# An expert layer's weights in units of 256 rows by 1024 columns, the expert width in two halves, and the small splits pinned behind weight splits

## The chip, the cores and the metric

The kernel runs on one core of one Trainium2 chip. The metric is the device time of one execution in microseconds (us). A core has five engines that run their own instruction streams in order: PE (TensorE, matrix products and transposes), DVE (VectorE), ACT (ScalarE), POOL (GpSimd) and SP (SyncE, which issues transfers here). They wait for each other through semaphores; 16 DMA engines move data between the chip's memory (DRAM) and the on-chip memory (SBUF). PE writes its sums into PSUM, which has banks of 512 f32 numbers in each of 128 partitions.

## The reference

One encoder block: a mixer (Fourier, convolution, gates, output projection), then a mixture of experts, then a norm. The change touches the experts alone. Shapes: 1024 tokens, model width 1024, 16 experts of width 2048; each expert picks the 128 tokens with its highest router probabilities.

```python
def expert_choice_moe(h, w_router, b_router, w_gate_e, w_up_e, w_down_e):
    b, s, d = h.shape
    cap = EC_CAPACITY * s // N_EXPERTS
    ...
    vals, idx = lax.top_k(jnp.swapaxes(probs, 1, 2), cap)
    xe = jax.vmap(lambda hb, ib: hb[ib])(h, idx)
    a = jnp.einsum('becd,edf->becf', xe, w_gate_e)
    u = jnp.einsum('becd,edf->becf', xe, w_up_e)
    y = jnp.einsum('becf,efd->becd', jax.nn.silu(a) * u, w_down_e)
    y = y * vals[..., None].astype(y.dtype)
    ...
```

The result is added to x, multiplied by a gate (gate_f), and a final RMS norm with the gain g_final follows. All weights are f32, and every expert reads 24 MB of them.

## The kernel before

**The work.** From 775.8 us to 1930 us of the profiled execution the program runs the experts, one after the other. Products are made in three parts for precision: a weight w is split into whi (ACT rounds it to a shorter format, L92, 128x1024 numbers at a time) and wlo = w - whi (DVE, L93); the token rows are split alike into xh and xl, the hidden rows into hth and htl. PE then adds whi·xh, whi·xl and wlo·xh (`mm3x`, L1300 to L1302; L106, L109 and L112 for the down weights).

**Units and chunks.** Weights come in units of 1 MB, issued by SP (`fetch`, L1120) into a ring of 12 buffers as soon as a buffer is free. A unit is two *chunks* of 128x1024. An expert has 48 chunks (16 gate, 16 up, 16 down), and each chunk gives PE six products of 512 columns, 288 in an expert. This text numbers the chunks of an expert c0 to c47. There are six buffers each for whi and wlo (NWB), so the split of chunk n+6 must wait until PE has finished chunk n; a split engine can be at most six chunks ahead of PE.

**The order before.** The width of 2048 is worked in four quarters of 512 (`fc`): a gate product into PSUM tile a, an up product into u (each one bank, two buffers), ACT's Silu of a, DVE's multiplication by u (h, L1244). Then `put` transposes the four 128-column pieces of h on PE into tp (L1205), which ACT and DVE split into hth and htl, and `down` adds the quarter's four chunks into y (two banks). Gate and up units hold 512 rows by 512 columns, down units 256 rows by 1024. During an expert, the next expert's tokens are found: `pick` compares positions (oh, L1068, DVE), makes indices by eight small products (L1075, PE), copies them (r, idx), and POOL gathers the rows (L1087); `turn` transposes them (L1104) and splits them into xh and xl, which the next expert's first products read. `ys` (L1269) scales an expert's result, which POOL adds to the rows in DRAM. In the first two experts (e0, e1) DVE also does the router's search for the other 14 (L1006 to L1052). In the last (e15), three units of down weights are used without a split, as plain f32 products (L1222), and the final norm of the rows not picked is done beside it (`final`, ACT's squares at L1313).

**What sets the order.** A scheduler of the language orders each engine's instructions by program order and priorities; `issue_after(i)` keeps an instruction behind instruction i, where that is written. Before, the multiplication h, the splits of transposed tiles and ys are not pinned.

Of the kernel before, what the change touches and what calls it, by code (L numbers as in the profile page):

```python
# [15 lines left out]
P = 128  # L16
# [12 lines left out]
NSH = 0  # L29
NCMP = 2  # L30
FIN = ((10, 0), (8, 2), (6, 4), (4, 6))
# [49 lines left out]
class Block:  # L81
# [578 lines left out]
    def rstd(self, pool, ss, name):  # L660
        nc = self.nc
        n = ss.shape[1]
        ms = pool.tile([P, n], F32, name=name + "ms")
        nc.vector.tensor_scalar(ms, ss, 1.0 / D, EPS, op0=OP.mult, op1=OP.add)
        rs = pool.tile([P, n], F32, name=name + "rs", bufs=2)
        nc.gpsimd.tensor_tensor(rs, ms, self.neghalf[:, 0:n], op=OP.pow)
        return rs
# [395 lines left out]
    def pick(self, pool, e):  # L1063
# [16 lines left out]
        if not e:  # L1080
            self.warm(lambda: self.pau.tile([P, 512], F32, name="u"), 22)
# [57 lines left out]
    def plain(self, rows):  # L1139

        raw = self.take().rearrange("p (i k n) -> p i k n", i=2, k=rows // 2)
        for i in range(2):
            yield raw[:, i]
            if i:
                self.fetch()
            self.step()

    def unit(self, rows):

        raw = self.take()  # L1150
        nc = self.nc
        for i in range(2):
            hi = self.wsp.tile([P, 1024], F32R, name="whi")
            lo = self.wsp.tile([P, 1024], F32R, name="wlo")
            src = raw[:, 1024 * i:1024 * i + 1024]
# [4 lines left out]
            elif self.npop < NWB:  # L1160
                with self.tc.issue_after(self.hold):
                    self.split(hi, lo, src)
            else:
                self.split(hi, lo, src)
            self.npop += 1
            if i:
                if self.npop <= NWS:
                    with self.tc.issue_after(self.gather):
                        self.fetch(nc.gpsimd)
                else:  # L1170
                    self.fetch()
            self.pin = self.last
            self.step()
            yield hi.rearrange("p (k n) -> p k n", k=rows // 2), lo.rearrange("p (k n) -> p k n", k=rows // 2)

    def expert(self, pool, e, picked, side):
# [6 lines left out]
        y = self.py.tile([P, D], F32, name="y")  # L1183

        def up(fc, name):
            ps = self.pau.tile([P, 512], F32, name=name)
            k = 0
            for b in range(2):
                for j, (wh, wl) in enumerate(self.unit(4)):
                    if self.npop > NWB and (j == 0 or self.ranked < 2):  # L1190
                        with self.tc.issue_after(self.hold):
                            next(side, None)
                    for i in range(2):
                        self.mm3x(ps, (xh[:, k, :], xl[:, k, :]), (wh[:, i, :], wl[:, i, :]), k == 0, k == KD - 1)
                        k += 1
                if self.left:
                    self.left.pop()()
            return ps

        def put(fc):  # L1200

            pt = self.ptp.tile([P, 4, P], F32, name="tp")
            h = hs.pop(fc)
            for i in range(4):
                nc.tensor.transpose(pt[:, i, :], h[:, i * P:(i + 1) * P], self.ident)  # L1205
            hf = None
            if last and fc in (1, 2):
                hf = pool.tile([P, 4, P], F32, name="htf")
                nc.scalar.activation(hf, pt, AF.Copy)
                if fc == 2:  # L1210
                    ht[fc] = (None, None, hf)
                    return
            hh = pool.tile([P, 4, P], F32R, name="hth", bufs=2)
            hl = pool.tile([P, 4, P], F32R, name="htl", bufs=2)
            self.split(hh, hl, pt)
            ht[fc] = (hh, hl, hf)

        def down(fc, b):
            if last and (fc, b) in ((1, 1), (2, 0), (2, 1)):
                for i, w in enumerate(self.plain(2)):  # L1220
                    for n in (0, 512):
                        nc.tensor.matmul(y[:, n:n + 512], lhsT=ht[fc][2][:, 2 * b + i, :], rhs=w[:, 0, n:n + 512],  # L1222
                                         start=False, stop=False)
                return
            for i, (wh, wl) in enumerate(self.unit(2)):
                if i == 0:
                    next(side, None)
                f = 4 * fc + 2 * b + i
                self.mm3([y[:, 0:512], y[:, 512:1024]], [t[:, 2 * b + i, :] for t in ht[fc][0:2]],
                         [(wh[:, 0, n:n + 512], wl[:, 0, n:n + 512]) for n in (0, 512)],  # L1230
                         first=(f == 0), last=(f == 15))

        for fc in range(4):
            pa = up(fc, "a")
            if last and fc == 0:
                self.gl = pool.tile([P, D], F32, name="ys")
                nc.gpsimd.dma_start(out=self.gl, in_=self.io["g_final"].rearrange("(o d) -> o d", o=1)
                                    .partition_broadcast(P))
            if fc:
                put(fc - 1)  # L1240
            pu = up(fc, "u")
            h = pool.tile([P, 512], F32, name="h", bufs=2)
# [258 lines left out]
```

## Time and profile before

| what | value |
|---|---|
| three runs | 1945.67, 1948.66, 1950.64 us; median 1948.66 us |
| profiled execution | 1944.46 us, span 1942.6 us |
| mean granted TensorE clock | 0.992 of full speed |
| PE busy | 1888.7 us, 97% of the span |
| DVE busy | 1583.4 us, 82% |
| ACT busy | 1117.6 us, 58% |
| experts e0 to e15 | 775.8 to 1930.2 us |

The span is the profiled execution from its first to its last instruction; the 1.9 us that its own time has beyond it lie around it. A matmul's busy time includes time in which it waits in PE's pipeline, so a PE that is 97% busy can still be held up; what a product costs is read from the distance of two starts.

### The profile page before, as it was taken

The page shows a single profiled execution, that of the slowest core. Times are in us where ns is not written, and L with a number is a line of the kernel's source. Part 1 is how long each engine was busy: PE and PEld are TensorE (multiplying, and loading weights), DVE is VectorE, ACT ScalarE, POOL GpSimd, SP SyncE. Part 2 cuts the span into 40 slices and gives each one's busy share as a digit, 9 for nine tenths or more (in the row PEclk, how much of TensorE's full clock was granted, in tenths as well). Part 3 has the DMA queues.
Part 4 walks back from the last instruction along what each step waited for, and adds up shares of the span by engine and source line. Part 5 has one row for each costly group of instructions (what it writes and reads, how often), then busy time and mean ns, then how long its engine had stood idle before and what let it go on. Part 6 is the DMA issues. An engine that isn't in the chain of part 4 may idle for free.

```text
span 1942.6 us, 23945 instructions
## 1 busy us (share of the span) xinstructions
PE 1888.7 (97%) x8777; PEld 1507.7 (78%) x8777; DVE 1583.4 (82%) x2005; ACT 1117.6 (58%) x1403; POOL 136.2 (7%) x124
## 2 busy tenths in 40 slices
PE   6999999999999999999999999999999999999996
PEld 5788888777788877777888777777778778777873
DVE  5976678676853767999999898898998999989886
ACT  5533233433510433776787777777767777677764
POOL 1000000000130111000000000000000000000001
PEclk9999999999999999999999999999999999999998
DMA  8322224465774842999999999999999999999993
GB/s 298 128 67 65 87 76 154 143 228 195 232 250 140 291 180 108 396 367 346 378 372 389 354 359 376 372 364 360 392 364 355 386 366 361 380 373 355 392 367 135
DMA packets 244746, 549.02 MB, mean 283 GB/s; under 512 B 12644, under 2 KB 51652, under 8 KB 244628
## 3 DMA queue, kind: packets, MB, share of 16 engines
q1 hardware_dynamic: 229248, 494.50, 69.8%
q0 software_dynamic: 14528, 52.75, 8.6%
q8 instruction: 69, 1.13, 0.2%
q10 hardware_dynamic: 852, 0.24, 0.1%
q14 instruction: 49, 0.40, 0.1%
HBM read 507.61 MB, written 39.86 MB: 282 GB/s over the span
## 4 chain that ended last, share of the span: by engine, by line
PE 76%; DVE 12%; DMA 5%; issue 4%; ACT 2%; POOL 0%; ACTq 0%; POOLq 0%; DVEq 0%
PE pb L315 9%; DVE wlo L93 7%; PE pa L315 6%; PE pc L315 6%; PE u L1302 5%; PE u L1300 5%; PE u L1301 5%; PE y L106 5%; PE y L109 4%; PE y L112 4%; PE a L1302 4%; PE a L1301 4%; PE a L1300 4%; DMA raw<-in_w_up_e_dram 3%; PE mm L106 3%
## 5 line engine op out<-in xcount | busy, mean ns | idle before, releaser
L93 DVE TENSOR_TENSOR wlo<-raw,whi 128x1024 fp32r<-128x1024 f32 x759 | 889.0, 1218 | 61.1 <-ACT whi L92 52.5
L92 ACT ACTIVATE whi<-raw 128x1024 fp32r<-128x1024 f32 x759 | 751.4, 1052 | 61.2 <-PE y L112 21.6
L1302 PE MATMUL a<-wlo,xh 128*128 128x512 f32 x512 | 206.2, 403 | 7.0 <-DVE wlo L93 5.7
L1302 PE MATMUL u<-wlo,xh 128*128 128x512 f32 x512 | 203.6, 398 | 2.4 <-DVE wlo L93 2.4
L1300 PE MATMUL u<-whi,xh 128*128 128x512 f32 x512 | 202.5, 395 | 1.6 <-ACT whi L92 1.6
L1300 PE MATMUL a<-whi,xh 128*128 128x512 f32 x512 | 201.5, 394 | 1.9 <-ACT whi L92 1.6
L1301 PE MATMUL a<-whi,xl 128*128 128x512 f32 x512 | 201.8, 394 | 0.0
L1301 PE MATMUL u<-whi,xl 128*128 128x512 f32 x512 | 201.8, 394 | 0.0
L109 PE MATMUL y<-wlo,hth 128*128 128x512 f32 x496 | 161.3, 406 | 0.5 <-DVE wlo L93 0.3
L106 PE MATMUL y<-whi,hth 128*128 128x512 f32 x496 | 159.5, 402 | 0.0
L112 PE MATMUL y<-whi,htl 128*128 128x512 f32 x496 | 156.4, 396 | 0.0
L92 ACT ACTIVATE wh<-s 128x512 fp32r<-128x512 f32 x80 | 50.3, 631 | 135.9 <-PE pc L315 76.0
L1302 PEld LDWEIGHTS a<-wlo,xh 128*128 128x128 f32 x512 | 96.4, 188 | 39.3 <-DVE wlo L93 19.8
L1302 PEld LDWEIGHTS u<-wlo,xh 128*128 128x128 f32 x512 | 96.3, 188 | 31.1 <-DVE wlo L93 8.0
L1300 PEld LDWEIGHTS a<-whi,xh 128*128 128x128 f32 x512 | 96.7, 189 | 21.9 <-ACT whi L92 2.5
L1301 PEld LDWEIGHTS a<-whi,xl 128*128 128x128 f32 x512 | 96.5, 188 | 22.0 <-DVE xl L93 0.4
L1300 PEld LDWEIGHTS u<-whi,xh 128*128 128x128 f32 x512 | 96.5, 188 | 21.0 <-ACT whi L92 2.6
L1301 PEld LDWEIGHTS u<-whi,xl 128*128 128x128 f32 x512 | 96.6, 189 | 20.5
L112 PEld LDWEIGHTS y<-whi,htl 128*128 128x128 f32 x496 | 93.4, 189 | 22.5
L106 PEld LDWEIGHTS y<-whi,hth 128*128 128x128 f32 x496 | 91.8, 189 | 20.9 <-issue 0.5
L109 PEld LDWEIGHTS y<-wlo,hth 128*128 128x128 f32 x496 | 89.9, 190 | 20.4 <-DVE wlo L93 2.4
L1243 ACT ACTIVATE h<-a 128x512 f32<-128x512 f32 x64 | 38.2, 596 | 106.6 <-PE a L1302 106.6
(530 smaller groups left out, 3183.1 us busy)
## 6 DMA issues: line engine op xcount, KB each, us to landing
raw<-in_w_gate_e_dram SPq DMA_DIRECT2D x126, 1024.0 KB, 7.2
raw<-in_w_up_e_dram SPq DMA_DIRECT2D x126, 1024.0 KB, 9.1
raw<-in_w_down_e_dram SPq DMA_DIRECT2D x126, 1024.0 KB, 8.1
ld<-in_w_ada_dram SPq DMA_DIRECT2D x48, 512.0 KB, 5.4
ld<-in_w_in_dram SPq DMA_DIRECT2D x44, 512.0 KB, 4.4
sg_d<-q POOLq DMA_DIRECT2D x8, 1024.0 KB, 6.1
ld<-sg_d SPq DMA_DIRECT2D x16, 512.0 KB, 4.9
x<-in_x_dram SPq DMA_DIRECT2D x8, 512.0 KB, 3.3
```

The lines of the kernel that those rows point to most:

```text
L92: a = self.nc.scalar.activation(hi, src, AF.Copy).ins
L93: self.last = a, self.nc.vector.tensor_tensor(lo, src, hi, op=OP.subtract).ins
L106: nc.tensor.matmul(o, lhsT=lh, rhs=rh, start=first, stop=False)
L109: nc.tensor.matmul(o, lhsT=lh, rhs=rl, start=False, stop=False)
L112: nc.tensor.matmul(o, lhsT=ll, rhs=rh, start=False, stop=last)
L315: nc.tensor.matmul(o, lhsT=x[:, k, :], rhs=y[:, k, :], start=first and k == 0 and i == 0, stop=last and k == 3 and i == 2, skip_group_chec ...
L1243: nc.scalar.activation(h, pa, AF.Silu)
L1300: nc.tensor.matmul(o, lhsT=lhs[0], rhs=rhs[0], start=first, stop=False, **kw)
L1301: nc.tensor.matmul(o, lhsT=lhs[1], rhs=rhs[0], start=False, stop=False, **kw)
L1302: nc.tensor.matmul(o, lhsT=lhs[0], rhs=rhs[1], start=False, stop=last, **kw)
```

## The change

All units become 256 rows by 1024 columns (`self.ulist`). The expert width is worked in two halves of 1024: gate half 0 in c0 to c7, up half 0 in c8 to c15, gate half 1 in c16 to c23, up half 1 in c24 to c31, then all of down in c32 to c47. Tiles a and u are two banks wide with one buffer each. `products` lets one set of token or hidden columns act on both 512-column halves of a chunk before the next set. `next` and `half` keep a queue of six split chunks ahead of the products. Silu, the multiplication h, the splits of transposed tiles and ys are put off by one or two chunks (`put_off`) and then pinned behind the splits made by then (`pinned`). Two quarters of transposes stand in c22, two in c38; the pick at c26; the turn at c42 (TURN) and c43. In the last expert the three plain units come in one run, and the multiplication of the last columns by g_final stands behind the norm's factor. `fetch` follows when a unit's second chunk has been split, or when a plain unit has been used.

```diff
-FIN = ((10, 0), (8, 2), (6, 4), (4, 6))
+FIN = ((8, 0), (7, 2), (5, 4), (4, 6))
+PLAIN = ((1, 1), (2, 0), (2, 1))
...
+        self.late = [(n - 1, f) for n, f in self.late]
+        due = [f for n, f in self.late if n <= 0]
+        self.late = [(n, f) for n, f in self.late if n > 0]
+        for f in due:
+            self.pinned(f)
+
+    def pinned(self, f):
+        with self.tc.issue_after(self.pin[0]), self.tc.issue_after(self.pin[1]):
+            return f()
...
+    def next(self):
+
+        while len(self.queue) < NWB and self.nunit < len(self.plan):
+            self.half()
+        self.nused += 1
+        return self.queue.pop(0)
...
+        def products(o, lhs, w, first, end):
+
+            wh, wl = w
+            for i, (x, y) in enumerate(((lhs[0], wh), (lhs[1], wh), (lhs[0], wl))):
+                for a, b in cols:
+                    nc.tensor.matmul(o[:, a:b], lhsT=x, rhs=y[:, a:b], start=first and i == 0, stop=end and i == 2)
...
+            self.put_off(1, split)
...
+            pa = up("a", gaps[0])
+            h = pool.tile([P, D], F32, name="h")
+            hs[f] = h
+            self.put_off(1, lambda: nc.scalar.activation(h, pa, AF.Silu))
+            pu = up("u", gaps[1])
+            self.put_off(1, lambda: nc.vector.tensor_tensor(h, pu, h, op=OP.mult))
...
+        gate_up(0, ({}, {0: gain} if last else {}))
+        gate_up(1, ({3: lambda: put(0), 4: lambda: put(1), 6: rows if last else lambda: None}, {}))
...
+            if k == 0 and not last:
+                picking()
+            if k in (3, 6):
+                put(2 + k // 6)
+            if k == TURN and not last:
+                hold["next"] = self.turn(pool, *hold["next"])
...
-            dn = [("w_down_e", e, 256 * b, 256 * b + 256, 0, D) for b in range(8)]
-            for f in range(4):
-                self.ulist += [(n, e, 512 * b, 512 * b + 512, 512 * f, 512 * f + 512)
-                               for n in ("w_gate_e", "w_up_e") for b in range(2)]
+            self.ulist += [(n, e, 256 * b, 256 * b + 256, D * f, D * f + D) for f in range(2)
+                           for n in ("w_gate_e", "w_up_e") for b in range(4)]
+            self.ulist += [("w_down_e", e, 256 * b, 256 * b + 256, 0, D) for b in range(8)]
...
-        gpau, self.pau = pool("pau", bufs=2, space=PSUM)
+        gpau, self.pau = pool("pau", space=PSUM)
```

On DVE, in a whole expert of the steady part (e8, from ys to the next expert's ys), the order before is this. The names are those above; xN at the end is N such instructions in a row.

```order
L1269 SCALAR_TENSOR_TENSOR ys<-y,val,gf 128x1024
L93 TENSOR_TENSOR wlo<-raw,whi 128x1024 x7
L1244 TENSOR_TENSOR h<-u,h 128x512
L93 TENSOR_TENSOR wlo<-raw,whi 128x1024 x3
L93 TENSOR_TENSOR htl<-tp,hth 128x512
L93 TENSOR_TENSOR wlo<-raw,whi 128x1024 x2
L1077 COPY r_11730<-tp 128x5
L1083 SCALAR_TENSOR_TENSOR idx<-r_11730 128x1
L1093 TENSOR_REDUCE val<-r_11730 128x1
L1068 TENSOR_TENSOR oh<-pos,slot 128x1024
L93 TENSOR_TENSOR wlo<-raw,whi 128x1024 x3
L1244 TENSOR_TENSOR h<-u,h 128x512
```

The first h stands behind the split of c8, although the product u that it reads ends with PE's c7; ys stands between the splits of c1 and c2. With the change the same stretch of DVE reads:

```order
L1305 SCALAR_TENSOR_TENSOR ys<-y,val,gf 128x1024
L95 TENSOR_TENSOR wlo<-raw,whi 128x1024 x15
L1264 TENSOR_TENSOR h<-u,h 128x1024
L95 TENSOR_TENSOR wlo<-raw,whi 128x1024 x4
L95 TENSOR_TENSOR htl<-tp,hth 128x512
L95 TENSOR_TENSOR wlo<-raw,whi 128x1024
L95 TENSOR_TENSOR htl<-tp,hth 128x512
L95 TENSOR_TENSOR wlo<-raw,whi 128x1024
L1079 COPY r_11245<-tp 128x5
L1085 SCALAR_TENSOR_TENSOR idx<-r_11245 128x1
L95 TENSOR_TENSOR wlo<-raw,whi 128x1024 x2
```

Here ys stands behind the split of c6, and h behind that of c21, whose buffer is free only when PE has finished c15, the last chunk of u; the second h stands in the same way behind c37. The copy r stands behind c27, and its eight small products on PE at the end of c26.

The second place is DVE in e1, where the router's search ends and the tokens of e2 are picked. Before:

```order
L1052 TENSOR_TENSOR pos<-pos,po_2_7361 128x8x14
L93 TENSOR_TENSOR wlo<-raw,whi 128x1024
L1068 TENSOR_TENSOR oh<-pos,slot 128x1024
L93 TENSOR_TENSOR wlo<-raw,whi 128x1024
L1077 COPY r_7369<-tp 128x5
L93 TENSOR_TENSOR wlo<-raw,whi 128x1024
L1083 SCALAR_TENSOR_TENSOR idx<-r_7369 128x1
```

The splits in these rows are those of c29, c30 and c31; PE's small products for this pick stand in c28, its turn of the rows in c44. With the change:

```order
L1054 TENSOR_TENSOR pos<-pos,po_2_7530 128x8x14
L95 TENSOR_TENSOR wlo<-raw,whi 128x1024
L1070 TENSOR_TENSOR oh<-pos,slot 128x1024
L95 TENSOR_TENSOR wlo<-raw,whi 128x1024
L1079 COPY r_7567<-tp 128x5
L95 TENSOR_TENSOR wlo<-raw,whi 128x1024
L1085 SCALAR_TENSOR_TENSOR idx<-r_7567 128x1
L1095 TENSOR_REDUCE val<-r_7567 128x1
```

They are now the splits of c38, c39 and c40; PE's small products stand in c39, the turn begins in c42.

The third place is ACT in the last expert, beside the first plain products. Before, from the Silu ahead of them:

```order
L1243 ACTIVATE h<-a 128x512
L92 ACTIVATE whi<-raw 128x1024 x3
L1313 ACTIVATE oh,ss_16244<-raw 128x1024
L92 ACTIVATE whi<-raw 128x1024
L1313 ACTIVATE oh,ss_16244<-raw 128x1024
L1209 ACTIVATE htf<-tp 128x512
L92 ACTIVATE whi<-raw 128x1024
L1313 ACTIVATE oh,ss_16285<-raw 128x1024
L92 ACTIVATE whi<-raw 128x1024
L1313 ACTIVATE oh,ss_16285<-raw 128x1024
L92 ACTIVATE whi<-raw 128x1024 x2
L1243 ACTIVATE h<-a 128x512
```

The copy htf reads transposes that PE makes between plain products, and the splits of the next gate chunks (c30 on) stand behind it and between squares. With the change:

```order
L1262 ACTIVATE h<-a 128x1024
L94 ACTIVATE whi<-raw 128x1024 x3
L1357 ACTIVATE oh,ss_16101<-raw 128x1024
L94 ACTIVATE whi<-raw 128x1024
L1357 ACTIVATE oh,ss_16101<-raw 128x1024
L94 ACTIVATE whi<-raw 128x1024
L1357 ACTIVATE oh,ss_16130<-raw 128x1024
L94 ACTIVATE whi<-raw 128x1024
L1357 ACTIVATE oh,ss_16130<-raw 128x1024
L94 ACTIVATE whi<-raw 128x1024 x2
L1357 ACTIVATE oh,ss_16183<-raw 128x1024 x2
L1357 ACTIVATE oh,ss_16210<-raw 128x1024
```

The last two splits in these rows are those of c36 and c37; behind them PE has its twelve plain products, and the next split (c38) follows two copies of transposes.

## Rows read from the trace of the kernel before

**Rows 1.** The page: busy time, share of the span, instructions.
```profile
PE 1888.7 (97%) x8777; PEld 1507.7 (78%) x8777; DVE 1583.4 (82%) x2005; ACT 1117.6 (58%) x1403; POOL 136.2 (7%) x124
```

**Rows 2.** Windows of e0, e1, e3, e4, e6, e15: five engines' busy, clock, DMA, GB/s.
```profile
775.80:849.60 73.80, 73.68 (x401) 57.79 (x402) 72.20 (x115) 55.76 (x59) 1.32 (x1) 1.00 1.04 394
849.60:928.40 78.80, 75.57 (x372) 58.88 (x371) 75.69 (x104) 55.25 (x58) 5.43 (x2) 0.96 0.98 349
...
997.80:1067.10 69.30, 69.30 (x321) 56.59 (x320) 63.92 (x63) 53.41 (x58) 3.86 (x2) 1.00 1.03 376
1067.10:1137.20 70.10, 69.64 (x322) 56.34 (x320) 61.73 (x62) 49.60 (x57) 3.62 (x2) 1.00 1.00 357
...
1208.20:1279.20 71.00, 70.27 (x322) 56.10 (x321) 64.10 (x64) 51.48 (x59) 3.62 (x2) 1.00 1.01 369
...
1846.40:1930.20 83.80, 76.43 (x299) 54.48 (x297) 66.49 (x67) 52.69 (x69) 8.46 (x7) 0.96 0.77 282
```

**Rows 3.** Waits of PE's weight loads, e5 to e13: total us, times, longest.
```profile
PEld a L1302 <- DVE wlo L93: 14.2, 27, 0.9
```

**Rows 4.** Timeline of DVE in e9: start, us, instruction, idle time before.
```profile
1422.56 1.28 DVE L1269 SCALAR_TENSOR_TENSOR ys<-y,val,gf 128x1024 f32<-128x1024 f32 x1
...
1433.15 0.69 DVE L1244 TENSOR_TENSOR h<-u,h 128x512 f32<-128x512 f32 x1 [0.44 <-PE u L1302]
```

**Rows 5.** DVE's groups in e6: busy us, mean ns | idle before.
```profile
L93 DVE TENSOR_TENSOR wlo<-raw,whi 128x1024 fp32r<-128x1024 f32 x49 | 56.9, 1217 | 3.8 <-ACT whi L92 3.8
L1244 DVE TENSOR_TENSOR h<-u,h 128x512 f32<-128x512 f32 x4 | 2.8, 691 | 1.7 <-PE u L1302 1.7
L1068 DVE TENSOR_TENSOR oh<-pos,slot 128x1024 bf16<-128x1024 f32 x1 | 1.2, 1218 | 0.0
```

**Rows 6.** Timeline of PE in e3, a stretch without waits.
```profile
1051.65 0.39 PE L1302 MATMUL u<-wlo,xh 128*128 128x512 f32 x1
...
1054.40 0.40 PE L1302 MATMUL u<-wlo,xh 128*128 128x512 f32 x1
...
1057.79 0.72 PE L106 MATMUL y<-whi,hth 128*128 128x512 f32 x2
1058.35 0.63 PE L109 MATMUL y<-wlo,hth 128*128 128x512 f32 x2
...
1063.02 0.62 PE L112 MATMUL y<-whi,htl 128*128 128x512 f32 x2
```

**Rows 7.** Timeline of PE in the output projection, ahead of the experts.
```profile
737.65 0.63 PE L109 MATMUL mm<-wol,zh 128*128 128x512 f32 x2
...
739.94 0.39 PE L106 MATMUL mm<-woh,zh 128*128 128x512 f32 x1
```

**Rows 8.** The pick in e1: timelines of PE, DVE, POOL; a window; gather transfers.
```profile
895.75 0.38 PE L1075 MATMUL tp<-v,oh 128*128 128x5 bf16 x8 [2.85 <-DVE oh L1068]
...
897.96 0.15 DVE L1083 SCALAR_TENSOR_TENSOR idx<-r 128x1 int32<-128x1 f32 x1
...
898.87 3.04 POOL L1087 DMA_INDIRECT xg<-h_d,idx  x1 [43.62 <-issue]
...
896.00:902.00 6.00, 6.00 (x22) 4.53 (x20) 5.21 (x9) 1.65 (x2) 3.04 (x1) 0.52 0.90 326
...
DMA to landing us min/median/max: 4.6/7.6/8.7
```

**Rows 9.** e15: timelines of ACT and PE, and a window.
```profile
1891.13 3.60 PE L1222 MATMUL y<-raw,htf 128*128 128x512 f32 x8
...
1894.77 0.60 ACT L1209 ACTIVATE htf<-tp 128x512 f32<-128x512 f32 x1 [7.00 <-PE y L1222]
...
1896.36 0.50 PE L1300 MATMUL a<-whi,xh 128*128 128x512 f32 x1 [1.63 <-ACT whi L92]
...
1899.00:1902.00 3.00, 2.90 (x7) 1.79 (x7) 2.59 (x4) 2.23 (x4) 0.31 (x1) 0.52 0.83 332
```

**Rows 10.** Timeline of DVE behind the last product.
```profile
1931.99 0.42 DVE L1289 TENSOR_TENSOR xg<-xg,ys 128x256 f32<-128x256 f32 x1 [0.63 <-ACT h L1288]
```

More of the change, by code (lines that the diff above doesn't have):

```diff
@@ L1200, in put @@
[L1200 to L1242, printed above, removed]
-            nc.scalar.activation(h, pa, AF.Silu)
-            nc.vector.tensor_tensor(h, pu, h, op=OP.mult)
-            hs[fc] = h
-            if fc == 1:
-                if last:
-                    xg = pool.tile([P, D], F32, name="xg")
-                    nc.gpsimd.indirect_dma_start(out=xg, out_offset=None, in_=self.x2_d,
-                                                 in_offset=bass.IndirectOffsetOnAxis(ap=idx[:, 0:1], axis=0))
-                else:
-                    while self.ranked < e + 2:
-                        next(side, None)
-                    with self.tc.issue_after(self.after):
-                        nxt = self.pick(pool, e + 1)
-            if fc:
-                down(fc - 1, 0)
-                if fc == 3:
-                    put(3)
-                down(fc - 1, 1)
@@ new lines, in gate_up, with picking @@
+        def gate_up(f, gaps):
+            pa = up("a", gaps[0])
[4 more added lines that the diff above has]
+            self.put_off(1, lambda: nc.vector.tensor_tensor(h, pu, h, op=OP.mult))
+        def picking():
+            while self.ranked < e + 2:
+                next(side, None)
+            with self.tc.issue_after(self.after):
+                hold["next"] = self.pick(pool, e + 1)
@@ L1273, in add @@
                 self.scattered = e == NE - 2
-            self.left.append(add)
-            return nxt
-        w = list(self.unit(2))
+            self.put_off(2, out)
+            return hold["next"]
+        xg = hold["xg"]
+        w = [self.next() for _ in range(2)]
         for _ in range(8):
@@ L1419, in run @@
         self.nfetch, self.npop, self.units, self.rows = 0, 0, [], []
+        self.plan = []
+        for e in range(NE):
+            self.plan += [False] * 16 + [e == NE - 1 and (b // 2, b % 2) in PLAIN for b in range(8)]
+        self.nunit, self.nhalf, self.nfree, self.nused, self.queue, self.read = 0, 0, 0, 0, [], set()
+        self.late = []
         def last():
```

155 lines of the change are left out of this document (100 added, 55 removed).

## The prediction

> **What bounds the kernel now.** The page's list of busy times comes first: PE is busy in 97% of the span, DVE in 82%, ACT in 58% [rows 1]. So time can only come from stretches in which PE waits, or from fewer or faster products. A table of windows, one per expert, shows where these are [rows 2]. From left to right a row has its bounds, its length, the busy time of PE, PE's loads, DVE, ACT and POOL, the granted clock, the DMA share and GB/s. e2 and e3 take 69.3 us each with PE always busy; e4 and e14 70.1; the nine experts e5 to e13 71.0 each, so 1.7 us more for the same products. e0 takes 73.8, e1 78.8 and e15 83.8 us, though e15 has six chunks of plain products in place of split ones.
>
> The view of waits tells whom PE waits for in e5 to e13: its largest row is wlo, 27 times at products into a, so three per expert, 14.2 us in all as its loads see it, each under 1 us [rows 3]. wlo is DVE's. But DVE works 64.1 of these 71.0 us [rows 2]; it is not short of time, it is short of it at some places. Its timeline shows them [rows 4]: the multiplication h waits 0.44 us for PE's last product into u, and by then DVE can't be more than a chunk ahead of PE, since it stands behind the split of c8 and reads a product that ends with c7. What follows h on DVE (splits, the pick's oh) has to make up for that. ys, 1.28 us, stands between the splits of c1 and c2 when DVE has just made xl. PE's loss is behind these places, at c2, c14 and c22.
>
> **The change, part by part.** DVE's work hardly changes: 48 weight splits, six small splits, oh and ys stay; four multiplications of 691 ns become two of twice the columns [rows 5]. PE has the same 288 products of 512 columns.
>
> *The place of h and ys.* h now stands behind the split of c21, whose buffer already needed PE's c15; so h waits for nothing, and DVE keeps what lead it has. With a split at 56.9/49 = 1.16 us [rows 5] and a chunk at six products of 0.23 = 1.38 us [rows 6], DVE gains 0.22 us of lead per chunk. I followed a steady expert by hand. Between c46 and c21 stand 23 chunks and ys: 23 x 0.22 - 1.28 = 3.8 us gained. At c21 h takes about 1.3 us, as two of 691 ns, and leaves 2.5. Two htl of 0.7 and the copy r come next; r waits for PE's small products at the end of c26, so DVE stands about 2 us there, and c28, c29 and oh (1.22) take 3.5 us while PE runs two and a half chunks. c30 comes within 0.3 us of its need, on either side; then lead is rebuilt to some 1.5 us at c37, enough for the second h. Transposes, with their splits, wait on PE, but at c25 and c40 DVE's wait falls in its own spare time (69.3 - 64.1 = 5.2 us). So the four waits go: e5 to e13 fall from 71.0 to 69.35, 9 x 1.65 = 14.85, and e4 and e14 lose 0.7 each: -16.2 us. If the cover at c30 is gone, 0.3 us come back per expert, +4 us over 14; I take 0.
>
> *Fewer turns of PE away from the weights.* The first product pair after four transposes starts its successor 0.56 us later, where a pair takes 0.466 [rows 6]: 0.09 us each. Seven such visits per expert become five: 2 x 0.09 x 14 = -2.5 us.
>
> *The order of products.* Products into one bank start 2.75/12 = 0.2292 us apart, pairs into the two banks of y 4.67/20 = 0.2335 each [rows 6]. Gate and up now also go in pairs into two banks. But pairs in the output projection, two halves under one weight set as well, run at 2.29/10 = 0.229 [rows 7]. So the price is 0 to 4.3 ns for 192 products in each of 16 experts: 0 to 13.2 us. y is the nearer row, with the same weight buffers beside the same splits; I take 3.7 ns, close to that end: +11.4 us.
>
> *e0 and e1.* Here DVE is the bound, since the search for the other 14 experts is on it. PE waited 2.85 us for oh in e1, and then ran at clock 0.52 (1.2 GHz) for 6 us, which costs half of that [rows 8]; with some waits for wlo behind it 6.9 us. These go, since oh now stands behind c38, in DVE's own flow. But idx comes nine splits (10.3 us) and some 1.1 us of h and htl later, at about 909.4 in place of 897.96; POOL begins 0.9 us after it and the rows land 7.6 to 8.7 us behind that [rows 8], so at about 918. PE reaches the turn at c42.5, two chunks after c40's split, near 912.7. It waits 5.3 us, and half speed follows again, 2.6 us: +7.9 - 6.9 = +1.0 (from -4 to +4). In later experts idx is there at c27 and the rows at c35, ahead of c42.
>
> *e15.* The copy htf keeps ACT waiting 7.00 us for transposes between plain products; the next weight splits on ACT stand behind it and among squares, so PE waits 1.63 us for whi, 0.53 for wlo, and then runs at 0.52 of full clock for some 3 us [rows 9]; the same returns 10 us later. How much this is in all follows from the length: 42 split chunks of 1.38 us, 24 plain products of 0.43 (eight take 3.60, of which the last ones' pipeline is 0.2 [rows 9]) and some 1.5 us of transposes make 69.8 of the 83.8 us. Of the 14 us of waiting about 2.6 stay, at the last columns and the start; 11.4 can go. With the change all plain products stand behind c37's splits, and give ACT and DVE 24 x 0.43 = 10.3 us to catch up. Four squares of 1.05 us among the splits of c32 to c37 come out of a lead of six chunks. I take -11 (from -7 to -13).
>
> *The tail.* DVE multiplies the last columns by g_final, 0.42 us, between ACT's sum and the norm's factor, after 0.63 us of wait [rows 10]; it moves behind the factor, where POOL's power hides it: about -0.7.
>
> *Units of 256 rows.* Bytes and the number of transfers stay, rows of 4 KB take the place of 2 KB. Transfers move 369 GB/s in a steady expert and 394 in e0 [rows 2], and PE waits for none. Cost 0. The Trainium skill, "DMA: Bandwidth & Descriptors", Specifications, gives about 358 GB/s from HBM to one core. By that an expert's 25.17 MB need 70.3 us, and no expert could be shorter. This trace disagrees: e2 and e3 read as much in 69.3, and e0's rate is 394.
>
> The sum: -16.2 - 2.5 + 11.4 + 1.0 - 11 - 0.7 = -18.0 us. Of the profiled 1944.5 us that leaves 1926.5; set against the median of 1948.66, 4.2 above the profile, 1930.6.
>
> **The rivals.** *The waits come back elsewhere.* ACT is held at hth behind c25 until the transposes in c22 are done, DVE at r until c26, and both are behind pinned orders. If these use up DVE's 5 us of spare time, a steady expert stays at 71.0. Then -2.5 is hidden, the slower pace too, and e15, tail and e0/e1 give -10.7: 1938. With the slower pace on top of the same waits, +9, the end is 1947, no change. Against it: the hand count finds about 3 us of such waits. *Transfers become the bound* as PE gets faster. At 70.3 us, nine experts gain 0.7 each, e2 and e3 lose 1 each: -6.3 + 2 - 10.7 = -15, 1934, with waits for raw that the trace before hardly has. *Slower.* The chain of split c21, h, transposes, hth, htl lies in order on DVE, PE and ACT. If DVE comes to c21 with less than 1 us of lead, PE waits for h in c22, and the split of c22 is late too: 1.3 + 1.16 - 1.38 = 1.1 us, twice an expert, with the r and oh place as much again: 3.3 us over 69.35, 72.65 per expert. That is 1.65 more than now in nine experts, 3.3 more in e2 and e3, 2.55 more in e4 and e14, +26.6; with -10.7 from the rest +15.9, 1964.6. It decides from (16.2 + 10.7) / 13 = 2.1 us per expert. DVE's 5.2 us of spare time speak against it.
>
> **How the numbers follow.** Forecast 0.68, with its own range 1917 to 1938 (pace 0 to 4.3 ns, c30, e0/e1 and e15 at their bounds). Waits elsewhere 0.17, of which half ends within 0.3% of the median; transfers 0.1; slower 0.05. A change under 0.3% (5.8 us) can't be told from none here. Faster: 0.68 + 0.1 + 0.07 = 0.85; same 0.1; slower 0.05. The range runs from 1916 to 1942.
>
> **What the profile would show.** Right: e5 to e13 alike and near 69.3 plus the pace, no wait of PE for wlo in them; h on DVE without a wait; starts of a and u products 0.23 or 0.2335 apart; one wait of about 5 us at the turn in e1; e15 near 72 us. Wrong: PE's waits at c22, c30 or c44; PE waiting for raw; products into a or u held by Silu or h, as these tiles have one buffer; e15 with a half-clock stretch.

## The result and the profile after

The changed kernel takes 1932.38 us in the median of five runs (1930.04 to 1937.25), the kernel before 1948.03 us (1945.67 to 1950.64) beside it. The ratio is 0.9923 with a 95% interval of 0.9903 to 0.9942: 0.8% faster. The prediction had set 0.3% as the least that can be told from no change. The profiled execution took 1933.76 us, with a span of 1932.0. The page's busy times, as in [rows 1]:

```profile
PE 1883.5 (97%) x8777; PEld 1517.6 (79%) x8777; DVE 1575.3 (82%) x1973; ACT 1136.2 (59%) x1371; POOL 312.2 (16%) x124
```

PE's and DVE's shares are what they were; only POOL has more than twice its time, to which the text comes back. The windows of e0, e1, e3, e6 and e15, with the columns of [rows 2], show where the time came from:

```profile
780.00:852.40 72.40, 72.39 (x393) 57.80 (x394) 70.76 (x106) 56.46 (x58) 1.30 (x1) 1.00 1.02 407
852.40:934.80 82.40, 74.47 (x380) 58.66 (x379) 75.60 (x109) 55.01 (x57) 6.69 (x2) 0.96 0.89 328
...
1004.70:1074.50 69.80, 69.80 (x321) 56.76 (x320) 61.45 (x59) 52.75 (x56) 3.62 (x2) 1.00 0.97 355
...
1214.30:1284.20 69.90, 69.90 (x321) 56.78 (x320) 63.62 (x62) 53.08 (x58) 18.33 (x2) 1.00 0.98 375
...
1843.40:1919.90 76.50, 72.76 (x299) 54.13 (x297) 65.37 (x65) 52.47 (x66) 22.38 (x7) 0.99 0.81 308
```

Every expert from e2 to e14 now takes 69.8 to 69.9 us with PE busy all through. Set against [rows 2]: e5 to e13 are 1.1 us shorter each, e2 and e3 0.5 longer, e0 1.4 shorter, e1 3.6 longer, e15 7.3 shorter. The experts begin at 780.0 us in place of 775.8. Ahead of them PE and ACT run the same instructions in the same order, and DVE does but for a shift of one or two. I take the 4.2 us as a difference between two executions: in the profiles of eleven kernels that share this stretch (the changed one and ten of the experiments) the experts begin at 777.6 to 788.0 us. They are why the profiles differ by 10.7 us and the medians by 15.65, and why the total of a single run tells less below than the lengths of its experts. From the first expert to the end of the span it is 1166.8 before (1942.6 - 775.8) and 1152.0 after: -14.8 us.

In e5 to e13 PE waits for no weight split any more; the view of waits has one row for its loads. The second fence has DVE's two largest waits in the same stretch:

```profile
PEld L1077 <- issue: 2.4, 9, 0.3
```

```profile
DVE htl L95 <- ACT hth L94: 21.6, 9, 2.4
DVE r L1079 <- PE tp L1077: 18.6, 9, 2.1
```

DVE has some 6 us of idle time per expert, about as much as before, and PE feels none of it. What has gone is the wait of h for PE, 0.44 us in [rows 4] and 1.7 us an expert in [rows 5]. The timeline of DVE in e9 shows h with no wait, and its whole wait at r:

```profile
1430.05 1.28 DVE L1305 SCALAR_TENSOR_TENSOR ys<-y,val,gf 128x1024 f32<-128x1024 f32 x1
1431.24 17.24 DVE L95 TENSOR_TENSOR wlo<-raw,whi 128x1024 fp32r<-128x1024 f32 x15
1448.40 1.22 DVE L1264 TENSOR_TENSOR h<-u,h 128x1024 f32<-128x1024 f32 x1
...
1462.53 0.17 DVE L1079 COPY r<-tp 128x5 f32<-128x5 f32 x1 [2.06 <-PE tp L1077]
```

PE's timeline in e9 shows both paces of [rows 6]. From 1424.02 to 1425.89 there are eight products, 1.87/8 = 0.234 us each; from 1464.28 to 1467.02, in the second up half, twelve in 2.74, 0.228 each, in the same order of products:

```profile
1424.02 0.63 PE L1225 MATMUL a<-whi,xh 128*128 128x512 f32 x2
...
1425.89 0.63 PE L1225 MATMUL a<-whi,xl 128*128 128x512 f32 x2
...
1464.28 0.62 PE L1225 MATMUL u<-whi,xh 128*128 128x512 f32 x2
...
1467.02 0.62 PE L1225 MATMUL u<-whi,xh 128*128 128x512 f32 x2
```

In e1, rows from the timelines of DVE, POOL and PE and one window answer to [rows 8]:

```profile
913.00 0.15 DVE L1085 SCALAR_TENSOR_TENSOR idx<-r 128x1 int32<-128x1 f32 x1
...
913.91 4.18 POOL L1089 DMA_INDIRECT xg<-h_d,idx  x1 [49.65 <-PE y L1225]
...
924.45 1.08 PE L1106 MATMUL tp<-ident,xg 128*128 128x128 f32 x4 [7.27 <-DMA xg<-h_d,idx]
...
924.00:929.00 5.00, 4.55 (x16) 3.88 (x17) 1.36 (x3) 2.14 (x3) 0.00 (x0) 0.57 0.38 153
```

The old wait for oh is gone; PE waits 7.27 us for the gathered rows, and then runs at 0.57 of full clock in the next 5 us.

In e15, rows of the waits of SP and ACT and of PE's timeline answer to [rows 9]:

```profile
SPq L1122 <- DMA x_d<-ys,idx: 20.2, 1, 20.2
...
ACT whi L94 <- DMA raw<-in_w_down_e_dram: 5.1, 3, 2.8
...
1898.29 0.73 PE L1225 MATMUL y<-wlo,hth 128*128 128x512 f32 x2 [0.74 <-DVE wlo L95]
...
1918.44 0.58 PE L1344 MATMUL y<-whi,hth 128*128 128x256 f32 x1 [1.64 <-DVE h L1325]
```

ACT's long wait for htf and the two half-clock stretches beside the plain products are gone. But SP stands 20.2 us at its first read of rows for the final norm, which must follow the scatter of e14; the down weights queue behind it, ACT waits 5.1 us for them, and PE waits for wlo at c36 and c37.

PE's longest wait, 1.64 us, stands at the last 256 columns, in the row at 1918.44. The same place in the kernel before, and then DVE's order ahead of it and a window with the change:

```profile
1929.19 0.39 PE L1300 MATMUL y<-whi,hth 128*128 128x256 f32 x1 [0.58 <-DVE h L1286]
```

```profile
1917.29 0.69 DVE L1331 TENSOR_TENSOR xg<-xg,ys 128x512 f32<-128x512 f32 x1 [0.79 <-ACT h L1328]
1917.90 0.48 DVE L1325 SCALAR_TENSOR_TENSOR h<-y,val,gf 128x256 f32<-128x256 f32 x1
...
1918.00:1920.00 2.00, 1.56 (x6) 1.36 (x6) 1.23 (x3) 0.51 (x2) 0.00 (x0) 0.54 0.11 45
```

At the last columns the change also fixes DVE's order, which the diff ahead of the prediction doesn't show:

```diff
-            nc.vector.tensor_tensor(xg[:, cs], xg[:, cs], self.gl[:, cs], op=OP.mult)
+            if n < 2:
+                with tc.issue_after(order):
+                    order = nc.vector.tensor_tensor(xg[:, cs], xg[:, cs], self.gl[:, cs], op=OP.mult).ins
```

The multiplication of the first 512 columns by g_final (L1331) now stands ahead of the next h (L1325), which is issued after `order`. It waits 0.79 us for ACT's square, h comes behind it, and PE waits 1.06 us longer than before. PE was busy for 1.77 us of the four from 1914 to 1918, and in the next two the granted clock is 0.54: a short half-clock stretch is there after all.

### The profile page after: what moved, and what is told of

It is laid out like the page before. It is cut to its first block, busy times and chain, and to the rows that moved or that the text cites. A ratio compares the mean times of both kernels' runs of the same rounds, so it can differ in the third digit from the quotient of the medians.

```text
span 1932.0 us, 24182 instructions
## 1 busy us (share of the span) xinstructions
PE 1883.5 (97%) x8777; PEld 1517.6 (79%) x8777; DVE 1575.3 (82%) x1973; ACT 1136.2 (59%) x1371; POOL 312.2 (16%) x124
## 4 chain that ended last, share of the span: by engine, by line
PE 88%; issue 4%; DVE 3%; DMA 2%; ACT 1%; POOL 1%; ACTq 0%; POOLq 0%; SPq 0%; DVEq 0%
PE a L1225 18%; PE u L1225 17%; PE y L1225 17%; PE pb L317 9%; PE pa L317 6%; PE pc L317 6%; PE mm L114 3%; PE mm L108 3%; PE mm L111 3%; PE tp L1240 1%; PE pa L191 1%; PE pb L191 1%; DMA raw<-in_w_down_e_dram 1%; DMA xg<-h_d,idx 1%; PE tp L1106 1%
## 5 line engine op out<-in xcount | busy, mean ns | idle before, releaser
L95 DVE TENSOR_TENSOR wlo<-raw,whi 128x1024 fp32r<-128x1024 f32 x759 | 883.8, 1218 | 20.3 <-ACT whi L94 18.5
L94 ACT ACTIVATE whi<-raw 128x1024 fp32r<-128x1024 f32 x759 | 777.6, 1059 | 143.5 <-PE a L1225 56.7
L1306 POOL DMA_INDIRECT x_d<-ys,idx x15 | 212.1, 14141 | 505.0 <-DVE ys L1305 479.1
L1225 PE MATMUL a<-whi,xl 128*128 128x512 f32 x512 | 162.4, 399 | 0.0
L1225 PE MATMUL a<-whi,xh 128*128 128x512 f32 x512 | 161.7, 397 | 0.2 <-ACT xh L94 0.2
L1225 PE MATMUL u<-wlo,xh 128*128 128x512 f32 x512 | 161.6, 397 | 0.0
L1225 PE MATMUL a<-wlo,xh 128*128 128x512 f32 x512 | 161.3, 397 | 0.0
L1225 PE MATMUL u<-whi,xh 128*128 128x512 f32 x512 | 160.5, 395 | 0.0
L1225 PE MATMUL u<-whi,xl 128*128 128x512 f32 x512 | 160.3, 394 | 0.0
L1225 PE MATMUL y<-wlo,hth 128*128 128x512 f32 x496 | 157.3, 397 | 1.4 <-DVE wlo L95 1.4
L1225 PEld LDWEIGHTS y<-whi,hth 128*128 128x128 f32 x496 | 91.8, 188 | 20.5 <-issue 0.5
```

The costliest lines, as they stand in the source:

```text
L94: a = self.nc.scalar.activation(hi, src, AF.Copy).ins
L95: self.last = a, self.nc.vector.tensor_tensor(lo, src, hi, op=OP.subtract).ins
L1225: nc.tensor.matmul(o[:, a:b], lhsT=x, rhs=y[:, a:b], start=first and i == 0, stop=end and i == 2)
L1306: nc.gpsimd.indirect_dma_start(out=self.x2_d, out_offset=bass.IndirectOffsetOnAxis(ap=idx[:, 0:1], axis=0), in_=ys, in_offset=None, comput ...
```

## The experiments

Lengths of experts below are distances from an expert's first gate product to the next expert's in PE's timeline (in e15, to its last product). Of the twelve kernels turn_c47 has four runs and best4 six; each of the others has one, which was profiled.

**h and ys where the scheduler puts them (h_free).** The changed kernel with Silu, h and ys neither put off nor pinned:

```diff
-            self.put_off(1, lambda: nc.scalar.activation(h, pa, AF.Silu))
+            nc.scalar.activation(h, pa, AF.Silu)
-            self.put_off(1, lambda: nc.vector.tensor_tensor(h, pu, h, op=OP.mult))
+            nc.vector.tensor_tensor(h, pu, h, op=OP.mult)
-            self.put_off(2, out)
+            out()
```

> Silu, h and ys are not put off and not pinned; units, halves and products stay. On DVE h then stands behind the splits of c15 and c33 (now c21 and c37), ys behind c1 (now c6). Theory (the place of h is the gain): h waits for the last product into u, and the next split is 1.3 + 1.16 - 0.92 = 1.5 us late, twice an expert; 69.9 becomes 72 to 73 us in 13 experts, the time 25 to 45 us longer than with the change. Rival (larger units and half the number of h and Silu instructions make the gain): within 0.3 us of 69.9.

It took 1964.51 us; e4 to e14 take 72.2 to 72.6 us, e2 and e3 stay at 69.3 and 69.8. DVE's timeline, and the waits of PE's loads from e5 on:

```profile
1461.13 1.23 DVE L1264 TENSOR_TENSOR h<-u,h 128x1024 f32<-128x1024 f32 x1 [2.29 <-PE u L1225]
...
PEld u L1225 <- DVE wlo L95: 19.7, 29, 1.1
PEld tp L1240 <- DVE h L1264: 9.0, 11, 0.8
```

Before its h DVE stands 2.29 us, and PE then waits for wlo and, at its transposes, for h. With all the large units and half the instructions the steady expert is slower than before the change. The place of h and ys together is worth 2.3 to 2.7 us an expert here (this run doesn't part the two), and the rival falls.

**No pins at all (no_pins).** What was put off comes at the same place of the program, but unpinned:

```diff
         for f in due:
-            self.pinned(f)
+            f()
```

> What is put off stays put off by one or two chunks in the program, but nothing is pinned behind a split. On DVE h stands behind the splits of c15 and c31, ys behind c47, the four htl behind c19, c21, c35 and c37. Theory (an instruction that waits for PE must stand six splits behind what it reads): h and ys now wait for products that end with the very chunk ahead of them, three times 1.5 us an expert, so 73 to 75 us in place of 69.90 and a time of 1975 to 2000 us. Rival (pins only fix an order that the scheduler would find as well): 69.9 to 70.5.

1982.44 us; a window of a steady expert, and DVE's waits in e5 to e13:

```profile
1227.50:1301.10 73.60, 70.84 (x322) 56.20 (x321) 63.71 (x61) 51.35 (x58) 3.63 (x2) 1.00 0.95 351
...
DVE h L1264 <- PE u L1225: 41.3, 18, 2.5
...
DVE ys L1305 <- PE y L1225: 14.6, 9, 1.6
```

DVE's work is the same 63.7 us; 73.6 us pass, since h waits 2.3 us for PE twice an expert and ys 1.6 once. Putting off alone doesn't keep h behind the splits that were made ahead of it; the pin does.

**The old kernel with h and ys later (old_h_ys_late).** The kernel before, quarters and 512-row units kept; in the loop that makes the splits, due functions are emitted and pinned behind the latest split:

```diff
-            nc.vector.tensor_tensor(h, pu, h, op=OP.mult)
...
+                self.late.append((3 if fc < 3 else 2,
+                                  lambda h=h, pu=pu: nc.vector.tensor_tensor(h, pu, h, op=OP.mult)))
...
-            self.left.append(add)
+            self.late.append((4, add))
```

> The kernel before, with its quarters, units and products, where only the multiplication h and ys are emitted later and pinned: h behind the splits of c10, c18, c30 and c41 (was c8, c16, c28, c40), ys behind c3 (was c1). Theory (their place alone made the waits): the waits at c14 and c22 go, that at c2 shrinks; e5 to e13 fall from 71.0 to 69.3 to 69.9 us, with gate and up at 0.229, the time by 10 to 15 us. Rival (it takes the two halves and fewer, larger instructions): 70.5 to 71.0.

1945.08 us, and 70.6 to 70.8 us in e5 to e13. A window, and the waits of PE's loads:

```profile
1284.60:1355.30 70.70, 70.22 (x322) 56.17 (x321) 64.32 (x64) 51.50 (x59) 4.44 (x2) 1.00 1.02 371
...
PEld u L1312 <- DVE wlo L93: 8.5, 18, 0.6
PEld y L109 <- DVE wlo L93: 7.1, 9, 0.8
```

The waits at c2, c14 and c22 are gone; new ones stand at c4 (behind ys at c3), c16 (behind oh at c15) and c24 (behind htl at c23). This is the rival's figure, not mine: h one or two splits later and ys two is not enough, where the change puts h six splits behind its product and gives oh a stretch of its own. Whether six splits would do it with the quarters kept was not tried. The h side of it is right (DVE waits for h no more), the price is what follows in the next places, where DVE has no lead yet.

**The order of products (one_bank, alt).** The changed kernel with, for one_bank, the three parts of one 512-column half before the other half, and for alt, banks changed at every product:

```diff
-            for i, (x, y) in enumerate(((lhs[0], wh), (lhs[1], wh), (lhs[0], wl))):
-                for a, b in cols:
+            t, z = ((lhs[0], wh), (lhs[1], wh), (lhs[0], wl)), [0, 0]
+            for n, i in ((0, 0), (0, 1), (0, 2), (1, 0), (1, 1), (1, 2)):
+                a, b = cols[n]
+                x, y = t[i]
```

(for alt the pairs are (0, 0), (1, 1), (0, 1), (1, 0), (0, 2), (1, 2)).

> Each chunk's three products go into one 512-column half before the other half, in gate, up and down. Theory (pairs over two banks of PSUM cost 4 ns a product): products start 0.229 us apart everywhere, where 39 of a steady expert's 48 chunks now run at 0.233; a steady expert falls from 69.90 to about 68.95 us, 39 x 6 x 0.0041, and the time by about 15 us. Since wlo is read 0.46 us earlier in a chunk, up to 0.3 us an expert may come back as a wait at c30. Rival (the pace has another cause, the 4 KB rows or the full engines beside it): 69.9 stays, plus that wait.

> Banks alternate with every product, and no set of token columns is loaded for two products in a row (xh, xl, xl, xh, xh, xh over the two banks; only the last two keep one set). If changing the bank costs: as now or a little slower, 69.9 to 70.2 us per steady expert. If the repeated use of one weight set costs: pace 0.229 and about 69.1 us. If neither: 69.9 with the same mix of 0.229 and 0.233.

1934.87 and 1936.06 us; the steady expert takes 69.91 and 69.90 us. PE's timeline in the first gate half, one_bank and then alt:

```profile
1429.98 0.40 PE L1227 MATMUL a<-whi,xh 128*128 128x512 f32 x1
...
1432.78 0.40 PE L1227 MATMUL a<-whi,xh 128*128 128x512 f32 x1
```

```profile
1430.01 0.40 PE L1227 MATMUL a<-whi,xh 128*128 128x512 f32 x1
...
1432.81 0.40 PE L1227 MATMUL a<-whi,xh 128*128 128x512 f32 x1
```

Both have twelve products in 2.80 us, 0.2333 each. So neither the change of bank nor the repeated use of one set of weights makes the slower pace, and my theory of it falls. Nor is it a property of these products in this kernel: in turn_c47 (below), which differs from the changed kernel by the turn of e1 alone, the first gate half of e2 has twelve products in 2.75 us, 0.229 each, and in the changed kernel's own e0 gate and up products start 0.229 apart as well.

```profile
926.26 0.62 PE L1225 MATMUL a<-whi,xh 128*128 128x512 f32 x2
...
929.01 0.62 PE L1225 MATMUL a<-whi,xh 128*128 128x512 f32 x2
```

**Rows of 2 KB (rows_2kb).** The changed kernel with each unit fetched in two column halves:

```diff
-        eng.dma_start(out=raw.rearrange("p (k n) -> p k n", k=k),
-                      in_=src[r0:r1, c0:c1].rearrange("(k p) n -> p k n", p=P))
+        for a in ((0, 512) if name else (0,)):
+            b = a + 512 if name else c1 - c0
+            eng.dma_start(out=raw.rearrange("p (k n) -> p k n", k=k)[:, :, a:b],
+                          in_=src[r0:r1, c0 + a:c0 + b].rearrange("(k p) n -> p k n", p=P))
```

> Each weight unit is fetched by two transfers of 256 rows by 512 columns, so rows of 2 KB as gate and up had before, and twice the transfers. If the unit's shape carries nothing: experts at 69.90 us, PE's pace in gate still 0.233. If rows of 4 KB slow PE's products: 0.229 in gate and up half 0, 69.4 us. If short rows were a cost that the change removed: waits for raw, over 70.5 us.

1937.24 us. The steady expert is the same to 0.01 us, with the same pace:

```profile
1218.60:1288.50 69.90, 69.90 (x322) 56.78 (x321) 63.66 (x62) 53.08 (x57) 18.36 (x2) 1.00 1.04 376
```

e0, e1 and e15 are some 1 us longer each (73.67, 83.33 and 77.52 us), in one run. The unit's shape carries nothing in the steady part and does not set the pace.

**The turn in e1 (turn_late, turn_c47).** The changed kernel with, in e1 alone, the turn at c47, as shown, or at c46 (14 in place of 15):

```diff
-            if k == TURN and not last:
+            if k == (15 if e == 1 else TURN) and not last:
```

> In e1 alone the turn stands at c46 in place of c42. Theory (the gather that lands late costs 7.3 us of waiting and a stretch at half clock): the wait falls by four chunks, 5.5 us, to about 1.8 us, and the half-clock stretch behind it goes or shrinks: e1 falls from 82.4 to 75 to 77 us, the rest unchanged, the time 6 to 8 us shorter. Rival (DVE bounds e1 by its search and the wait only hides that, so it comes back as waits for wlo): e1 stays above 80 us.

> The changed kernel with one edit: the turn in e1 stands at c47. e1 falls from 82.4 to 76.8 us, e2 stays within 0.5 us of 69.8, all else stays: 5 to 6 us below the changed kernel, 1926 to 1927 us by its median, and a ratio of 0.989 to the kernel before. If DVE's search bounded e1 all along, nothing is gained.

turn_late took 1928.3 us with e1 at 78.7: a smaller gain than I expected, since the wait fell by 3.6 us and not by 5.5. turn_c47, in four runs, takes 1926.6 us (1923.6 to 1929.97), at a ratio of 0.9895 (0.9876 to 0.9913) to the kernel before: the lowest median of this study, though its interval overlaps that of the change itself (0.9903 to 0.9942). Rows of the waits of PE in e1, for the turn at c46 and then at c47, and windows of e1 and e2 in the latter:

```profile
PE tp L1106 <- DMA xg<-h_d,idx: 3.7, 1, 3.7
```

```profile
PE tp L1106 <- DMA xg<-h_d,idx: 1.5, 1, 1.5
...
850.00:924.90 74.90, 72.75 (x381) 57.24 (x380) 74.51 (x107) 55.13 (x57) 6.70 (x2) 1.00 0.96 354
924.90:994.20 69.30, 69.30 (x322) 56.53 (x321) 66.83 (x65) 55.11 (x57) 10.13 (x2) 1.00 1.02 395
```

With a wait of 1.5 us the clock stays at 1.00, and e1 is 7.5 us shorter than with the change, e2 no longer.

**The end of e14 and the last expert (x_on_pool, ys14_early, best1, best4).** x_on_pool lets POOL issue the reads of rows:

```diff
-        eng = eng or self.nc.sync
...
+        eng = eng or (self.nc.sync if name else self.nc.gpsimd)
```

> The four reads of rows for the final norm are issued by POOL, not by SP. Theory (in the last expert SP waits 20.2 us at the first of these reads for the scatter of e14, and all weight units queue behind it): ACT's 5.1 us of waits for down weights go, and PE's waits at c36 to c42 with them; e15, 76.2 us to the last product, falls to 72 to 74 us, the rest stays. Rival (the squares and the final norm on ACT and DVE make e15 late, not the loads): e15 stays within 0.7 us.

1943.8 us, of which the experts' later start (786.2 in place of 780.0) is 6.2; e15 takes 80.1 us, 3.9 more than with the change, where I expected 2 to 4 less. The window of e15 to the last product, and ACT's wait in it:

```profile
1849.20:1930.30 81.10, 73.70 (x299) 53.14 (x297) 65.60 (x66) 52.48 (x66) 25.28 (x11) 1.00 0.78 291
...
ACT oh L1357 <- DMA raw<-x_d: 6.6, 2, 5.6
```

ACT's waits for weights are gone, as I expected, and it waits 6.6 us for the rows, which POOL reads only behind the gather of the last expert's rows; the squares stand among the weight splits on ACT, so PE is held up more. ys14_early moves ys of e14 alone:

```diff
-            self.put_off(2, out)
+            if e == NE - 2:
+                out()
+            else:
+                self.put_off(2, out)
```

> The changed kernel, where ys of e14 alone is neither put off nor pinned; it stands behind c1 of e15, as all did before, in place of c6. Theory (the scatter of e14 starts late and is slow, and SP's first read of rows, with the weight units behind it, waits 20.2 us for it): the scatter starts 6 us earlier and ends 6 to 12 us earlier, SP's wait falls to 8 to 14 us, and e15 from 76.2 to 73 to 75 us. A wait of PE at c2 of up to 0.7 us may come with it. Rival (squares pinned behind c32 to c35 make ACT and DVE late there): e15 within 0.7 us of 76.2.

1934.07 us, e15 76.16: nothing. POOL's and DVE's timelines:

```profile
1845.58 22.76 POOL L1306 DMA_INDIRECT x_d<-ys,idx  x1 [30.93 <-DVE ys L1305]
...
1845.22 22.92 DVE L95 TENSOR_TENSOR wlo<-raw,whi 128x1024 fp32r<-128x1024 f32 x20
```

The scatter begins 5.4 us earlier and takes 5.7 us longer, so it ends when it did, and SP waits 20.5 us for it.

best1 is x_on_pool with the turn of e1 at c47.

> The reads of rows on POOL and, in e1 alone, the turn at c47. Both theories hold: e1 near 77 us (78.7 with the turn at c46, less one chunk), e15 72 to 74 us, so 7 to 9 us below the change. If xl then comes late for e2's first products, e2 gains a wait of 1 to 2 us.

1941.99 us: e1 76.8 and e2 69.5 us as expected, e15 81.9 for the reason just told. best4 is the same with the reads of rows pinned ahead of the last expert's own row gather:

```diff
+        def behind():
+            with self.tc.issue_after(self.xd):
+                gain()
+                rows()
...
+        gate_up(0, ({}, {}))
+        gate_up(1, ({3: lambda: put(0), 4: lambda: put(1)}, {1: behind} if last else {}))
```

> The turn in e1 at c47, and the four reads of rows for the final norm on POOL directly behind the scatter of e14, ahead of the reads of g_final and of the last expert's own rows. Theory (SP's block of 20 us delays weights in e15, and on POOL it was the place behind the row gather that delayed the rows): neither ACT's waits for weights nor those for rows remain, e15 72 to 74.5 us, 7 to 10 us below the changed kernel. Rival (the scatter itself ends too late for the squares at c32 to c35, whichever queue reads): e15 76 us or more, no gain over the turn alone.

1930.64 us in six runs (ratio 0.9916, 0.9894 to 0.9938), 4 us more than turn_c47 beside it; e15 takes 78.0 us, 1.6 more than there. POOL's first read is its next instruction behind the scatter, 7.25 us after the scatter's end there, and ACT still waits for rows:

```profile
ACT oh L1364 <- DMA raw<-x_d: 6.8, 3, 3.4
```

The rival's figure came true: on either queue, the rows come too late for squares that stand among the splits of c32 to c37.

A late scatter is not all of it. In no_pins the scatter of e14 takes 2.32 us on POOL, SP waits 0.5 us for it, and ACT waits for neither rows nor weights:

```profile
SPq L1122 <- DMA x_d<-ys,idx: 0.5, 1, 0.5
```

Yet PE's 36 products of c32 to c37 take 9.78 us there, against 9.99 with the change, where 0.2335 each would be 8.41. The products of c36 and c37 are the late ones, 0.28 and 0.40 us apart, and in that run's other experts they start 0.233 apart. That points to the squares on ACT and the norm's multiplications on DVE among these splits, which hold PE up with the rows on time, too. DVE comes there with less lead in that run, since its h waits, so what the late scatter adds with the change stays open.

## Why the prediction was right, point by point

**The whole.** 1930.6 us was predicted and 1932.4 measured. Against the profile of before the sum was -18.0 us; between the two profiles the experts and what follows are 14.8 us shorter, so 3.2 us of the gain are missing, nearly all in e15.

**The place of h and ys, and the rest of e2 to e14.** Predicted was -16.2, with -2.3 for fewer turns and +9.2 for the pace in these 13 experts (13/14 of the one term and 13/16 of the other), -9.3. Measured is 918.0 us before (928.4 to 1846.4) and 908.6 after (934.8 to 1843.4): -9.4. That they agree so closely is in part luck: the pace cost some 7.7 us in place of 9.2 (below), so the waits and turns gave some 17.1 in place of 18.5. The mechanism is shown by two runs: without the late, pinned place of h and ys the expert takes 72.2 us or more (h_free) or 73.6 (no_pins), and PE's waits for wlo come back. In the old kernel a place that is only a little later gives 70.7 (old_h_ys_late). DVE's idle time at r was 2.06 us where the hand count had about 2. My count of c30 was right too: PE has no wait there.

**Fewer turns.** Five places in e9 have a pair that starts its successor 0.08 to 0.09 us late (c22, c26, c38, c42, c43), as counted.

**The pace.** The sum's size was right in its place, the reason that I gave was not. Gate and up run at 0.2333 us in c0 to c22 and at 0.229 in c23 to c31, so the term is 23 of 32 chunks and 4.3 ns, 0.6 us an expert in place of 0.7. But one_bank and alt keep the pace with other orders of banks and weights, rows_2kb with other rows, and e0 of the changed kernel and e2 of turn_c47 run the same products at 0.229. The step that failed is the price by the nearest row taken as a price of pairs over two banks. What sets the pace stays open; the trace shows that in a steady expert it changes behind the transposes of c22 and with the first product into y.

**e0 and e1.** Predicted +1.0, with the pace and turns of two experts about +2; measured 154.8 us after against 152.6 before, +2.2. idx came at 913.00, or 908.8 with the 4.2 us of the later start taken off, against 909.4; PE reached the turn where I put it, but waited 7.3 us, not 5.3: POOL's gather itself took 4.18 us in place of 3.04, and the rows were there 10.5 us after its start. In return e0 was 1.4 us shorter, where pace and turns would have made it 0.5 longer; its gate and up products ran at 0.229, and why the rest of it is shorter was not followed up. turn_c47 confirms the mechanism: the wait falls to 1.5 us, the half clock goes, and e1 is 7.5 us shorter.

**e15.** Predicted -11 and +0.7 for the pace; measured 83.8 to 76.5, -7.3. The removed part is right: no wait for htf, no 1.63 us at whi, no half clock beside the plain products. The term that was mis-sized is the waiting that stays, put at 2.6 us. PE's starts show 4.0 us more of it, in three places. The products of c32 to c37 take 9.99 us in place of 8.41; those of c40 and c41 3.20 in place of 2.80; and from the first product of the last columns to the start of the last one it is 6.84 us (1912.83 to 1919.67), where it was 4.82 before (1925.07 to 1929.89). The plain products, 0.4 us shorter than counted, give a little back.

At the last columns the cause is DVE's new order there, in which I had looked at the tail alone and not at h and PE behind the multiplication by g_final; the longer wait and the half clock behind it are most of these 2.0 us. At c36 and c37 I had put the cost of the squares at nothing, to be paid from a lead of six chunks, and had not counted DVE's multiplications of the final norm, 1.28 us each, between the splits of c34 to c37, so that the splits start 2.0 to 2.4 us apart there. And ys moved from c1 to c6: I followed it on DVE alone, and not the scatter behind it, POOL and SP, for which SP waits 20.2 us, so that rows and weights come late too. How the 2.0 us of the first two places divide between squares, multiplications and late transfers stays open. Neither another queue nor an earlier ys helped; what would shorten the scatter in the changed kernel was not tried, nor was the old order at the last columns.

**The tail.** Predicted -0.7, measured 12.4 to 12.1 us, -0.3. The new order of DVE at the last columns cost 1.06 us of waiting in e15, so there it lost more than it gained.

**The rivals.** Waits elsewhere: DVE's waits did move, to htl and r, 2.4 and 2.1 us an expert, and its spare time covers them. Transfers as the bound: experts of 69.9 us at 375 GB/s with no wait for raw. The Trainium skill, "DMA: Bandwidth & Descriptors", Specifications, gives some 358 GB/s to a core, or 70.3 us an expert by my estimate; the measured rate is above it and decides. Slower: PE waits nowhere in e5 to e13 for the chain behind the split of c21. Of the signs of being wrong one came, in small: a half-clock stretch in e15, at its end.

## What to carry to other kernels

Where an in-order engine makes work for a faster one, with a limited number of buffers, look for the instructions in its stream that wait for the fast engine. Here such an instruction was put as many buffers behind its input as there are, six, so that the buffer's own wait covers it. With h at c15 in place of c21, and ys at c1 in place of c6, the expert took 2.3 us of 70 longer; in the old kernel a place one or two splits later moved most of the wait to the next cluster. When an instruction is moved, follow what it triggers through each queue: here ys carried a scatter, the scatter a read on SP, and the read all weights behind it; and the multiplication by g_final, moved ahead of an h, held up that h and PE behind it. A result that comes late (e1's search) moves the wait to whatever hangs on it next, so that should stand as late as its reader allows.

## What the runs showed of the hardware

**A scatter's time on POOL.** The same scatter took 2.32 us before (at 1424.12) and 17.08 in the changed kernel, from 1431.60 in e9:

```profile
1431.60 17.08 POOL L1306 DMA_INDIRECT x_d<-ys,idx  x1 [36.61 <-DVE ys L1305]
```

It ends at 1448.68. Its end goes with the first break in DVE's run of splits. In e9 DVE runs without one for the first 15.62 us of the scatter, stands 0.04 us ahead of the last of the 15 splits, and the scatter ends 1.46 us after that. In ys14_early the first break comes after 21.29 us and the end 1.47 us later. In h_free, where the run is only eight splits long, the scatter takes 10.27 us and ends 1.47 us after the run:

```profile
1440.43 10.27 POOL L1306 DMA_INDIRECT x_d<-ys,idx  x1 [30.68 <-DVE ys L1305]
...
1440.07 9.17 DVE L95 TENSOR_TENSOR wlo<-raw,whi 128x1024 fp32r<-128x1024 f32 x8
1451.93 4.63 DVE L95 TENSOR_TENSOR wlo<-raw,whi 128x1024 fp32r<-128x1024 f32 x4 [2.69 <-ACT whi L94]
```

The Trainium skill, "SBUF — State Buffer", section "SBUF: two separate sides", says that POOL can't write a transfer's descriptors while DVE runs an operation in a mode that takes the port which the two share, and gives a copy as its case. DVE's splits here are subtractions, which are not that case. And in the kernel before, in no_pins and for e2's result in the changed kernel the scatter took 2.3 us beside unbroken runs of the same splits. That a run of DVE holds a scatter up until its first break is argued from the three ends above; what decides whether it does stays open.

**A pace that depends on the moment.** The same products, from the same buffers into the same PSUM tile, start 0.2333 us apart in one half of a steady expert and 0.229 in the other, at a granted clock of 1.00, and in e0, or in e2 of turn_c47, 0.229 apart in both.
